# Seven of 22 FFN-up column groups as seven half-size block products instead of eight, in a one-core hybrid decoder layer

## The chip, the cores and the metric

The kernel runs on one core of a Trainium2 chip. The metric is the device time of one execution in microseconds. Its engines are TensorE (PE, with the weight loads shown apart as PEld), VectorE (DVE), ScalarE (ACT), GpSimd (POOL) and SyncE (SP); SP issues the ordinary loads, POOL issues DMAs through a software queue, and both kinds of transfer run on the same 16 DMA engines.

## The reference, cut to what matters

One decoder layer with S = 512 tokens and D = 1024 channels: an input projection, two token mixers (sparse attention and gated DeltaNet), a gated merge with an output projection, a layer norm, and then the part that is changed, a gated MLP with a causal convolution of width 3 over the tokens, followed by a second layer norm. All is float32.

```
FFN_DIM = 2816
def conv_ffn(x, w_up, conv_w, w_down):
    h = causal_dwconv(x @ w_up, conv_w)          # w_up: 1024 x 5632
    gate, val = jnp.split(h, 2, axis=-1)
    return (jax.nn.silu(gate) * val) @ w_down    # w_down: 2816 x 1024
...
        x = layer_norm(DEEPNORM_ALPHA * x + mix, ln1_g[l], ln1_b[l])
        f = conv_ffn(x, ffn_w_up[l], ffn_conv_w[l], ffn_w_down[l])
        x = layer_norm(DEEPNORM_ALPHA * x + f, ln2_g[l], ln2_b[l])
```

## The kernel before

**Products.** Every float32 operand of a product is split in two: a high part rounded to fp32r (a copy on ACT, name `wh` for weights) and a low part, the difference (a subtraction on DVE, name `wl`). A product of one 128x128 weight block is three matmuls, high by high, high by low and low by high; in `product` these are lines 484, 486 and 487. The activations of the FFN lie in SBUF as `mh` and `ml`, 8 blocks of 128 channels by 512 tokens.

**Weights.** `split_w` loads a weight tile of 512 KB (`raw`, 128x1024, a ring of three), and splits it in two halves of 128x512. `wh` and `wl` are rings of three halves each, so ACT writes a new `wh` when PE has finished with the one three halves back.

**FFN-up.** The 2816 columns of each branch (gate and value) are 22 groups of 128, so the loop `for p in range(NF)` runs over p = 0 to 21, and inside over the branches b = 0, 1. One branch of one group is 8 blocks of 128 channels by three matmuls of 512 columns, 48 matmuls in a group; they accumulate in the PSUM bank `pu0` or `pu1`. The products of groups 0 and 1 are made earlier, interleaved with the layer norm, in matmuls of 256 columns. Behind each product comes the gated convolution: ACT reads the bank (`fa`, line 1407), DVE adds two shifted terms per branch (line 1410), ACT takes the tanh, DVE and POOL multiply (lines 1415 and 1416). The result `fth` is stored split as the operand of FFN-down (`ph`, `pl`), with block sums `sr`, lines 1420 to 1430.

**FFN-down** is already done as seven block products in place of eight (the scheme of Strassen and Winograd). It needs four sums of blocks of its weights, which are made in DRAM by accumulating DMAs that POOL issues: `sums(n)`, line 513, eight DMAs of 2816 KB into `wsum`. `ROUNDS` says at which group of FFN-up each of the later ones is written in the code. The output projection `w_o` is treated the same way, with eight DMAs of 1024 KB (`osum`, line 503) in the first stage.

**Order.** The order of the instructions of each engine is written out: `QUEUES` holds one list of numbers for PE, DVE, ACT, POOL and SP each, so the work of different groups is interleaved on an engine as the lists say, not as the loop reads.

```
ROUNDS = [2, 4, 6, 8, 10, 13, 15]
BUFS = {..., 'raw': 3, 'wh': 3, 'wl': 3, ...}
```

Of the kernel before, what the change touches and what calls it, by code (L numbers as in the profile page):

```python
# [129 lines left out]
ROUNDS = [2, 4, 6, 8, 10, 13, 15]  # L130
# [3 lines left out]
    "PE": """0-9 11-12 10 13-32 41 38 35-37 33 42-43 53 39 34 54 44-45 47-48 40 50-52 49 55 46 65 56-57 66 59-60 58 61-63 67 64  # L134
71-72 77-78 74 68 79 69 89 75-76 73 70 86 90 87 80 83 91 88 98 81-82 107 101 108 99 84 109-110 100 111 85 102 112 95
113-114 96 115 103 116-117 92 118-119 93 120-122 94 97 123-148 155-178 149-153 104-106 154 183-205 207 206 208-220
179-180 221-230 181-182 235-251 259-260 252-254 261 255 262-264 231 265-267 232 302 268-271 256 303 272 257-258 233
273 234 304-305 274-277 306-307 278-282 308 310 309 311 360 283-290 361 388 291-298 362-365 389-391 366 312-313
367-370 392 371-372 314-315 373-374 393 375-377 394 378 395 379-383 396 299-300 397-405 444-446 301 447 416 406-407
417 408-410 418-419 411 420-434 456 435-436 448-449 457 437-439 458 450 316-317 451 320-321 318 322-323 319 459-463  # L140
324-327 464-466 328 332-339 329-330 467 331 468-471 513 472 340-347 473 514 474-475 348-355 476-477 515 356-359 452
384-387 516 478 517 479 501-502 453-455 412-415 518 503 519-521 504 522-526 440-441 527 442-443 723-724 528-529
725-727 530-532 728-729 480 484 481-483 533-534 485 505-506 535-536 730 486 507-508 731-733 487 734-738 751 739
488-489 752 740 490 509 491 741-742 492 541-542 753 493-494 754 743 495 510 496 543 511 546 755 497 544-545 512 547
756-757 498-499 744 758 500 548 759-760 549-551 560-561 761 745 762-765 562 565-566 766 552 767 746 553 768 554 537
555 591-592 563-564 567 538 568-569 539-540 581-582 769 570 593-596 556 597 557 598 558 599-600 770-771 559 571 583
585-586 796-797 772 584 572 798 573-575 773 587 601-602 576 799 577 774 800 588-589 801-806 603 606 590 604 651 578
605 607 579-580 807-810 608 653 811 620-621 609-611 652 812-813 654 814 612 815-816 622 625-626 613 623-624 614-616
864-865 627-628 641 629-630 642 866-870 617-618 871 619 643 645 872 631 646 873 644 632-633 874 634 875 647 876-877
635-636 699-700 648 637 649-650 638-639 878 640 701 879 704 702 880 817 705 881 703 818 882-886 706 718-719 707-709  # L150
887 720-721 819 838-839 722 710 655 659-660 656-658 661-662 840 854-855 711-712 841 663-666 842-843 713-715 856
667-669 671-678 670 857-858 716-717 844-845 679-686 860-861 859 846 862 687-694 863 1053 847-848 695-698 747-750
936-940 1054 941 1055 775 1056 776 1057 849 777-778 850 942-944 779 945-948 780 949-951 781-782 1058 952-954 783-784
1059 955 977 785 978-979 956 786-787 980 957-959 981 1060 788 1072-1073 789-790 851 982-985 791-792 986-991 793-794
992-993 795 1061 994-999 852-853 1000-1007 1074 1008-1009 1062 1075-1076 820 824-825 1010-1011 1101 821-823 826-829
1012 1102 1063 1029 830 832-833 831 1030-1036 1013 1037-1040 1103-1108 834 1014 1041 835 1042-1043 1015 836 1044 837
888-889 1045-1052 1064-1065 1016 1066-1067 1017 1077-1082 890-891 1068 1083-1100 1069 1018 1109 1070 1110 1019 1111
1020-1021 1112 1022-1024 892-894 896 895 897-899 1071 1203 1205-1208 900-903 1209 1113 1204 1114-1115 1210 1219 1116
1220 1117-1118 904 1211 908-915 905-906 1221 907 1212-1214 1223 1215 1119-1121 1216 1224 916-923 1222 1217 1122
924-931 1218 1123 932-935 1225-1226 1233-1234 960 1227 1124-1125 1228 961 1126-1127 962-963 1128-1131 964-965 1235  # L160
1132-1133 966 1134 1141-1142 967-968 1135-1136 1143-1144 969-970 1238 1145-1149 971 1236 972 1150-1151 973 1239
1179-1180 1152 1181 974 1240-1243 1237 1153-1154 975-976 1155-1156 1182 1157 1252-1253 1158-1159 1183-1184 1160
1185-1187 1161 1244 1162-1164 1188 1245-1247 1025 1137 1248 1138 1254 1139-1140 1257 1259 1026 1258 1189-1198 1273
1283 1199 1027 1249 1255 1028 1256 1250 1200 1274 1201-1202 1165 1251 1166 1260 1284-1285 1169-1170 1167 1261-1262
1168 1307-1308 1286 1309-1311 1171-1173 1275 1174 1277-1278 1287 1312 1288 1313 1263 1314-1317 1175-1176 1276 1177
1279 1178 1264 1403 1289 1404 1318 1265-1266 1405 1280-1282 1267 1408 1268 1406-1407 1269 1319 1409 1270 1320 1271
1321-1323 1290 1324 1229 1272 1291-1293 1325 1410-1411 1231 1326-1330 1294-1295 1412-1413 1422 1296 1423 1230 1297
# [1404 lines left out]
```

## Time and profile before

| what | us |
|---|---|
| median of 3 runs (lowest 832.77, highest 833.51) | 833.2 |
| the profiled execution | 831.55 |
| its span, first to last instruction | 829.8 |
| PE busy in the span | 809.2 (98%) |
| DVE busy | 602.5 (73%) |
| ACT busy | 409.2 (49%) |
| POOL busy | 180.5 (22%) |

The mean granted clock of TensorE was 0.992. The profiled execution lies 1.65 us below the median, and 1.75 us of it are outside the span. By the code and the trace the stages are: both mixers and the merge to about 432 us; the output projection, the layer norm and the first two groups of FFN-up to about 493 us; the rest of FFN-up to about 724 us; FFN-down and the last layer norm to 829.8 us. A group of instructions in the profile is named by line, engine, operation and tile; `wl<-raw,wh` is the subtraction that makes the low part of a weight.

### The profile page before, as it was taken

Reading aid. Unit: us, or ns where it says so; the run is one execution under the profiler, and the core shown is the slowest. Engines: PE = TensorE matmul, PEld = TensorE weight load, DVE = VectorE, ACT = ScalarE, POOL = GpSimd, SP = SyncE. Lnnn points to the kernel's source line nnn. Section 1 sums busy time; section 2 is a strip of 40 time slices with the busy share of each in tenths; the row PEclk is TensorE's granted clock in tenths of the full one; section 3 lists DMA queues with packets and bytes.
Section 4 is the critical chain, followed back from the end, with each engine's and each line's share of the span. In section 5 each row is a group of like instructions: output and inputs, shape, how many; then the busy total and the mean of one; then the engine's idle time right before and its main releaser. Section 6 shows DMA issues by size and latency. Waiting matters only on the chain.

```text
span 829.8 us, 11767 instructions
## 1 busy us (share of the span) xinstructions
PE 809.2 (98%) x4138; PEld 673.8 (81%) x4138; DVE 602.5 (73%) x1339; ACT 409.2 (49%) x912; POOL 180.5 (22%) x176
## 2 busy tenths in 40 slices
...
GB/s 279 102 92 101 252 32 133 44 96 108 49 219 111 233 51 52 120 108 128 115 241 177 152 147 211 125 102 102 215 103 249 229 102 80 150 199 182 190 257 124
DMA packets 43979, 119.58 MB, mean 144 GB/s; under 512 B 3472, under 2 KB 4624, under 8 KB 43664
## 3 DMA queue, kind: packets, MB, share of 16 engines
...
q0 software_dynamic: 11776, 31.46, 16.3%
q8 instruction: 33, 0.54, 0.3%
...
HBM read 116.72 MB, written 33.55 MB: 181 GB/s over the span
## 4 chain that ended last, share of the span: by engine, by line
PE 82%; DVE 9%; DMA 4%; ACT 2%; issue 2%; POOL 1%; ACTq 0%; DVEq 0%; POOLq 0%; SPq 0%
PE pu L484 10%; PE pu L486 10%; PE pu L487 10%; PE gps L484 8%; PE gps L486 8%; PE gps L487 8%; DMA raw<-wsum 3%; PE pw L1288 3%; PE px L1452 3%; PE pu L1288 2%; PE pz L1452 2%; PE pout L1089 2%; PE pu L1452 2%; PE aps L1075 2%; PE pm L484 2%
## 5 line engine op out<-in xcount | busy, mean ns | idle before, releaser
L474 DVE TENSOR_TENSOR wl<-raw,wh 128x512 fp32r<-128x512 f32 x146 | 102.7, 705 | 78.0 <-ACT wh L470 38.6
L470 ACT ACTIVATE wh<-raw 128x512 fp32r<-128x512 f32 x126 | 79.1, 629 | 133.7 <-PE pu L486 97.0
L486 PE MATMUL pu<-ml,wh 128*128 128x512 f32 (+1 forms) x384 | 131.5, 373 | 0.0
L484 PE MATMUL pu<-mh,wh 128*128 128x512 f32 (+1 forms) x384 | 130.8, 372 | 0.4 <-ACT mh L1267 0.4
L487 PE MATMUL pu<-mh,wl 128*128 128x512 f32 (+1 forms) x384 | 130.8, 373 | 0.0
L484 PE MATMUL gps<-xh,wh 128*128 128x512 f32 x320 | 125.7, 404 | 3.2 <-ACT mt L1121 2.1
L486 PE MATMUL gps<-xl,wh 128*128 128x512 f32 x320 | 126.1, 401 | 0.0
L487 PE MATMUL gps<-xh,wl 128*128 128x512 f32 x320 | 124.4, 400 | 0.0
L484 PEld LDWEIGHTS pu<-mh,wh 128*128 128x128 f32 x384 | 71.3, 188 | 13.4 <-ACT mh L1267 0.7
L487 PEld LDWEIGHTS pu<-mh,wl 128*128 128x128 f32 x384 | 71.4, 188 | 13.0 <-DVE wl L474 0.5
L486 PEld LDWEIGHTS pu<-ml,wh 128*128 128x128 f32 x384 | 71.4, 188 | 12.6
L1410 DVE SCALAR_TENSOR_TENSOR fa<-pu,fcw,fa 128x511 f32<-128x511 f32 (+1 forms) x88 | 64.6, 744 | 17.5 <-ACT fa L1407 16.9
L1416 POOL TENSOR_TENSOR fth<-fth,fa 128x512 f32<-128x512 f32 x22 | 30.4, 1387 | 212.6 <-DVE fth L1415 186.3
L484 PEld LDWEIGHTS gps<-xh,wh 128*128 128x128 f32 x320 | 60.4, 190 | 15.1 <-issue 2.5
L487 PEld LDWEIGHTS gps<-xh,wl 128*128 128x128 f32 x320 | 60.8, 190 | 10.9
L486 PEld LDWEIGHTS gps<-xl,wh 128*128 128x128 f32 x320 | 61.0, 191 | 10.2
L1387 ACT ACTIVATE wh<-raw 128x512 fp32r<-128x512 f32 x67 | 40.1, 626 | 41.0 <-DMA raw<-in_down 13.5
L1388 DVE TENSOR_TENSOR wl<-raw,wh 128x512 fp32r<-128x512 f32 x67 | 44.8, 694 | 17.9 <-ACT wh L1387 17.3
L474 POOL TENSOR_TENSOR wl<-raw,wh 128x512 fp32r<-128x512 f32 x30 | 40.1, 1339 | 13.4 <-ACT wh L470 7.9
L525 POOL TENSOR_TENSOR rs<-rs,minus_half 128x1 f32<-128x1 f32 x8 | 7.2, 901 | 161.4 <-DVE rs L1246 161.4
L1407 ACT ACTIVATE fa<-pu,fcw 128x512 f32<-128x512 f32 x44 | 29.7, 680 | 24.8 <-PE pu L487 22.0
L1048 ACT ACTIVATE sc<-sc,mn 128x384 f32<-128x384 f32 (+2 forms) x64 | 35.7, 560 | 10.5 <-DVE mn L1046 10.1
(365 smaller groups left out, 1719.8 us busy)
## 6 DMA issues: line engine op xcount, KB each, us to landing
raw<-in_up SPq DMA_DIRECT2D x44, 512.0 KB, 3.7
raw<-in_wT SPq DMA_DIRECT2D x40, 512.0 KB, 3.6
wsum<-in_down POOLq DMA_DIRECT2D x6, 2816.0 KB, 20.8
raw<-wsum SPq DMA_DIRECT2D x20, 512.0 KB, 3.9
raw<-in_down SPq DMA_DIRECT2D x15, 512.0 KB, 4.3
...
wsum<-wsum POOLq DMA_DIRECT2D x2, 2816.0 KB, 14.6
raw<-in_wm SPq DMA_DIRECT2D x8, 512.0 KB, 3.5
```

What stands on the lines that cost most here:

```text
L470: A.activation(wh, r, AF.Copy)
L474: eng.tensor_tensor(wl, r, wh.bitcast(F32), op=OP.subtract)
L484: i = PE.matmul(ps, wh[k], mh_(k), start=(k == 0), stop=False)
L486: PE.matmul(ps, wh[k], ml_(k), start=False, stop=False)
L487: PE.matmul(ps, wl[k], mh_(k), start=False, stop=(k == n - 1))
L1048: A.activation(s[:, i, :n], s[:, i, :n], AF.Exp, scale=-1.0, bias=mn[:, 0, i:i + 1], accum_out=mn[:, 1, i:i + 1])
L1288: PE.matmul(ps[t], a[x](j)[:, ts], w[y][:, j % 2, :], start=fresh and j == 0 and i == 0, stop=j == TT - 1 and i == 2, skip_group_check=True)
L1387: A.activation(hi, raw[:, i], AF.Copy)
L1388: V.tensor_tensor(lo, raw[:, i], hi.bitcast(F32), op=OP.subtract)
L1410: V.scalar_tensor_tensor(acc[:, n:], ps[:, :S - n], w[:, i:i + 1], acc[:, n:], op0=OP.mult, op1=OP.add)
L1416: G.tensor_tensor(th, th, g[1], op=OP.mult)
L1452: m = PE.matmul(ps, a[x][:, j, ts], w[y], start=first and i == 0, stop=last and i == 2, skip_group_check=True)
```

## The change

Groups 5, 7, 9, 11, 13, 15 and 17 of FFN-up are taken as one product of 2x2 blocks each: the activations in two halves of the channels by two halves of the tokens (`x11`, `x12`, `x21`, `x22`, each 4 channel blocks by 256 tokens), the weights in two halves of the channels by the two branches. `seven(p)` makes seven products of 4 channel blocks by three matmuls of 256 columns, 84 matmuls of 256 columns in place of 48 of 512. It is a generator in four pieces that are written between the four half products of the plain group p - 1.

- Weights: of the seven weight blocks three are blocks of `ffn_w_up`, and four are sums, which eight accumulating DMAs of POOL prepare in DRAM for all seven groups (`sums_u`, 1.8 MB each). A group loads 1.75 MB in place of 1 MB and splits seven halves of 128x512 in place of four. Two of the four loads of a group go into a tile of its own, `raw7`, which has one buffer: weights 0 and 1 first, and later 4 and 5.
- Activations: `x_sums` makes four sums of blocks and splits them, once, written between groups 1 and 2: ten operations on DVE (six sums and four splits), two on POOL and four copies on ACT, all 128x1024.
- Results: partial results are combined in SBUF (`wf0`, `wf1`): four copies of 128x256 on ACT and three additions of 128x256 on DVE for a group. The gated convolution of these groups then reads SBUF in place of a PSUM bank.
- The tiles `ph`, `pl` and `sr` are cut in a part for 9 and a part for 2 of the 11 pairs of groups, the second of which is allocated when the tiles of the seven-product groups are freed; later pieces of `sr` are split 5, 4, 2 in place of 4, 4, 3.
- `ROUNDS` and all lists of `QUEUES` are new. The eight `wsum` DMAs move: before, three stood in the first stage and five in FFN-up; now all stand behind the first stage or in FFN-up, and the eight DMAs of `sums_u` stand in the first stage among those of `osum`.

```diff
-ROUNDS = [2, 4, 6, 8, 10, 13, 15]
+SEVEN = [5, 7, 9, 11, 13, 15, 17]
+NA = 9
+ROUNDS = [2, 4, 6, 8, 10, 12, 14]
...
 QUEUES = {
-    "PE": """0-9 11-12 10 13-32 41 38 35-37 33 42-43 53 39 34 54 44-45 47-48 40 50-52 49 55 46 65 56-57 66 59-60 58 61-63 67 64
...
+    usum = dr.tile([128, len(SEVEN), 4, S + 16], F32, name="usum")[:, :, :, :S]
+    def u_block(r, c):
+        a, n = SEVEN[0], len(SEVEN)
+        return d["up"][a:a + 2 * n:2, :, c, 4 * r:4 * r + 4, :].rearrange("u p k f -> p u (k f)")
+    def sums_u():
+        at = lambda i: usum[:, :, U_AT[i], :]
+        todo = [(0, u_block(0, 0), 0), (1, u_block(0, 1), 0), (0, u_block(0, 1), 1), (1, u_block(1, 1), 1),
+                (2, at(1), 0), (2, u_block(0, 0), 1), (3, at(2), 0), (3, u_block(1, 0), 1)]
+        for (to, src, add), u in zip(todo, SUMS_U):
+            i = G.dma_start(out=at(to), in_=src, **({"accum_op": OP.add} if add else {}))
...
+    def x_sums():
...
+        def parts_of(i, x):
+            A.activation(xs_[i][0], x, AF.Copy)
+            V.tensor_tensor(xs_[i][1], x, xs_[i][0].bitcast(F32), op=OP.subtract)
+        a, b, c, e = spare
+        G.tensor_tensor(a, hi(x11), lo(x11), op=OP.add)
+        V.tensor_tensor(b, hi(x21), lo(x21), op=OP.add)
+        V.tensor_tensor(c, b, hi(x22), op=OP.subtract)
+        V.tensor_tensor(c, c, lo(x22), op=OP.subtract)
+        parts_of(0, c)
+        V.tensor_tensor(e, c, a, op=OP.subtract)
+        parts_of(1, e)
+        G.tensor_tensor(b, a, b, op=OP.subtract)
+        parts_of(2, b)
+        V.tensor_tensor(c, e, hi(x12), op=OP.add)
+        V.tensor_tensor(c, c, lo(x12), op=OP.add)
+        parts_of(3, c)
...
+    def seven(p):
...
+        def weights(i):
+            if i % 2 == 0:
+                own = i in (0, 4)
+                raws[i] = raw = (sx if own else wp).tile([128, 2, 512], F32, name="raw7" if own else "raw",
+                                                         bufs=1 if own else BUFS["raw"])
...
+                if i == 0:
+                    nc.sync.dma_start(out=raw, in_=flat(0, 0, 8))
+                elif i == 2:
+                    nc.sync.dma_start(out=raw, in_=usum[:, n, 0:2, :])
+                elif i == 4:
+                    nc.sync.dma_start(out=raw[:, 0:1], in_=usum[:, n, 2:3, :])
+                    nc.sync.dma_start(out=raw[:, 1:2], in_=flat(1, 4, 8))
+                else:
+                    nc.sync.dma_start(out=raw[:, 0:1], in_=usum[:, n, 3:4, :])
...
+        mul(0, px, pure_(x11), True)
+        A.activation(f[0][:, left_], px[:, :256], AF.Copy)
+        yield
+        mul(1, py, pure_(x12), True)
+        V.tensor_tensor(f[0][:, left_], f[0][:, left_], py[:, :256], op=OP.add)
+        mul(2, px, sum_(1), False)
+        A.activation(f[1][:, left_], px[:, :256], AF.Copy, scale=-1.0)
+        yield
+        mul(3, pz, sum_(0), True)
+        A.activation(f[1][:, right_], pz[:, :256], AF.Copy)
+        mul(4, px, sum_(2), False)
+        V.tensor_tensor(f[1][:, right_], f[1][:, right_], px[:, :256], op=OP.subtract)
+        yield
+        mul(5, pz, sum_(3), False)
+        V.tensor_tensor(f[1][:, left_], f[1][:, left_], pz[:, :256], op=OP.add)
+        mul(6, px, pure_(x22), False)
+        A.activation(f[0][:, right_], px[:, :256], AF.Copy)
+        yield f
...
     for p in range(NF):
+        if p == NE:
+            x_sums()
         g = []
+        if p in SEVEN:
+            f = next(ahead)
+            g = [gated(p, b, f[b]) for b in range(2)]
+        elif p + 1 in SEVEN:
+            ahead = seven(p + 1)
         for b in range(2):
...
-                wu = split_w(d["up"][p, :, b], [128, KD, 128], V)
-                i = product(ps, wu, (lambda k: mh[:, k, :], lambda k: ml[:, k, :]), KD)
+                for half in range(2):
+                    if p + 1 in SEVEN and (b or half):
+                        next(ahead)
+                    i = plain(p, b, half, ps) or i
```

In the rows below the names are those of the code, with a number for the buffer; `waits` names the semaphores that an instruction waits for.

PE in the middle of FFN-up, before: the matmuls of one branch, in triples, with some of the next branch mixed in.

```order
L486 MATMUL pu_5744<-ml,wh 128x512
L487 MATMUL pu_5744<-mh,wl 128x512
L484 MATMUL pu_5744<-mh,wh 128x512
L486 MATMUL pu_5744<-ml,wh 128x512
L487 MATMUL pu_5744<-mh,wl 128x512
L487 MATMUL pu_5698<-mh,wl 128x512
```

PE in the middle of FFN-up, after: lines 1515 (the seven-product groups) and 1568 (plain groups).

```order
L1568 MATMUL pu_5920<-mh,wl 128x512
L1568 MATMUL pu_5920<-mh,wh 128x512
L1568 MATMUL pu_5920<-ml,wh 128x512
L1568 MATMUL pu_5920<-mh,wl 128x512
L1515 MATMUL px_5703<-ml,wh 128x256
L1515 MATMUL px_5703<-mh,wl 128x256
L1515 MATMUL px_5939<-mh,wh 128x256
L1515 MATMUL px_5939<-ml,wh 128x256
L1515 MATMUL px_5939<-mh,wl 128x256
```

Matmuls of 512 columns now alternate with runs of 256 columns that go to other banks.

DVE in the loop of FFN-up, before: low parts of weights (line 474) between the convolution terms (1410) and the gate (1415).

```order
L1410 SCALAR_TENSOR_TENSOR fa_6030<-pu_6004,fcw,fa_6030 128x511
L1415 SCALAR_TENSOR_TENSOR fth<-fth,fa_5942 128x512 [waits DVE_49]
L474 TENSOR_TENSOR wl<-raw,wh 128x512 [waits PE_49,Activation_49]
L1410 SCALAR_TENSOR_TENSOR fa_6069<-pu_6044,fcw,fa_6069 128x511
L1410 SCALAR_TENSOR_TENSOR fa_6069<-pu_6044,fcw,fa_6069 128x510 [waits DVE_49]
L1410 SCALAR_TENSOR_TENSOR fa_6030<-pu_6004,fcw,fa_6030 128x510
L474 TENSOR_TENSOR wl<-raw,wh 128x512 [waits DMAHW6_49,PE_49,Activation_49]
```

DVE in the loop of FFN-up, after: 1505 makes the low parts for a seven-product group (`raw_6056` is its weights 0 and 1 or 4 and 5 in `raw7`, `raw_6180` the next content of the same tile), 1563 those of a plain group, 1534, 1537 and 1527 are the additions into `wf`.

```order
L1505 TENSOR_TENSOR wl<-raw_6056,wh 128x512 [waits DMAHW5_49,PE_49,Activation_49]
L1563 TENSOR_TENSOR wl<-raw,wh 128x512 [waits PE_49,Activation_49]
L1505 TENSOR_TENSOR wl<-raw_6056,wh 128x512 [waits DMAHW6_49,PE_49,Activation_49]
L1534 TENSOR_TENSOR wf_5943<-wf_5943,px_5939 128x256 [waits PE_49]
L1505 TENSOR_TENSOR wl<-raw,wh 128x512 [waits DMAHW7_49,Activation_49]
L1607 SCALAR_TENSOR_TENSOR fth<-fth,fa_5903 128x512 [waits Activation_49]
L1563 TENSOR_TENSOR wl<-raw,wh 128x512 [waits DMAHW0_49,PE_49,Activation_49]
L1537 TENSOR_TENSOR wf_5943<-wf_5943,pz_5941 128x256
L1505 TENSOR_TENSOR wl<-raw_6180,wh 128x512 [waits DMAHW1_49,PE_49,Activation_49]
```

Seven low parts and three additions of a group are woven into the work of the plain group; between the last low part from one content of `raw7` and the first from the next stand five other instructions of DVE, two of them low parts.

POOL from the layer norm into FFN-up, before: one step of the inverse square root, then the gates `fth`, with two weight-sum DMAs among them.

```order
L525 TENSOR_TENSOR rs<-rs,minus_half 128x1 [waits DVE_49,Pool_49] x2
L513 DMA wsum_101<-in_down 1408x1x512 [waits DMASW2_49]
L1416 TENSOR_TENSOR fth<-fth,fa_5461 128x512 [waits DVE_49,Activation_49]
L1416 TENSOR_TENSOR fth<-fth,fa_5446 128x512
L513 DMA wsum_102<-wsum_101 1408x512 [waits DMASW3_49]
L1416 TENSOR_TENSOR fth<-fth,fa_5550 128x512 [waits DVE_49,Activation_49]
```

POOL in the same place, after: lines 1440 and 1447 are the two operations of `x_sums`, 1608 is the gate.

```order
L539 DMA wsum_101<-in_down 1408x1x512 [waits DMASW2_49,DMASW1_49]
L1440 TENSOR_TENSOR sr0a<-mh,ml 128x1024 [waits DMAHW1_49,DVE_49,DMAHW3_49,PE_49,Activation_49]
L1447 TENSOR_TENSOR sr1a<-sr0a,sr1a 128x1024 [waits DVE_49,Pool_49]
L1608 TENSOR_TENSOR fth<-fth,fa_5481 128x512 [waits DVE_49,Activation_49]
L539 DMA wsum_102<-wsum_101 1408x512 [waits DMASW2_49]
L1608 TENSOR_TENSOR fth<-fth,fa_5466 128x512
L1608 TENSOR_TENSOR fth<-fth,fa_5586 128x512 [waits DVE_49,Activation_49]
L539 DMA wsum_102<-in_down 1408x1x512 [waits DMASW4_49,DMASW3_49]
L1608 TENSOR_TENSOR fth<-fth,fa_5671 128x512 [waits DVE_49,Activation_49]
L1608 TENSOR_TENSOR fth<-fth,fa_5907 128x512 [waits DVE_49,Pool_49]
L539 DMA wsum_100<-in_down 1408x1x512 [waits DMASW0_49]
```

The weight-sum DMAs now follow one another with one to two gates between them in the first groups of FFN-up, where before the next one stood several gates on.

More of the change, by code (lines that the diff above doesn't have):

```diff
@@ L139 @@
[L139 to L143, printed above, removed]
@@ L517, in gemm_t @@
         ps = gps()
-        first = product(ps, w, (lambda k: xh[:, k, :], lambda k: xl[:, k, :]), KD)
+        FIRST[u] = first = product(ps, w, (lambda k: xh[:, k, :], lambda k: xl[:, k, :]), KD)
         if after is not None:
@@ L1142, in body @@
     sums_o()
+    sums_u()
     tail = ExitStack()
@@ L1369, in body @@
     pdn = psum("pdn", 1)
+    sxs = ExitStack()
+    sx = pool(sxs, name="sx", bufs=1, side="left")
+    xs_ = [tuple(sx.tile([128, 4, 256], F32R, name=f"s{x}{i}") for x in "hl") for i in range(4)]
+    x11, x12, x21, x22 = ((k, slice(256 * r, 256 * r + 256)) for r in range(2) for k in range(2))
+    def x_sums():
+        spare = [r.js(NA - 4, NA) for r in sr]
+        hi, lo = (lambda v: mh[:, 4 * v[0]:4 * v[0] + 4, v[1]].bitcast(F32)), (
+            lambda v: ml[:, 4 * v[0]:4 * v[0] + 4, v[1]].bitcast(F32))
+        def parts_of(i, x):
[14 more added lines that the diff above has]
+        parts_of(3, c)
     soon = []
@@ new lines, in gated, with plain @@
+    def gated(p, b, ps):
+        w = fcw[:, b * NF + p, :]
+        acc = fs.tile([128, S], F32, name=f"fa{b}", bufs=2)
+        A.activation(acc, ps, AF.Copy, scale=w[:, 2:3])
+        for i in (1, 0):
+            n = 2 - i
+            V.scalar_tensor_tensor(acc[:, n:], ps[:, :S - n], w[:, i:i + 1], acc[:, n:],
+                                   op0=OP.mult, op1=OP.add)
+        return acc
+    raws_ = {}
+    def plain(p, b, half, ps):
+        if half == 0:
+            raws_[b] = wp.tile([128, KD, 128], F32, name="raw", bufs=BUFS["raw"])
+            nc.sync.dma_start(out=raws_[b], in_=d["up"][p, :, b])
+        r = raws_[b][:, 4 * half:4 * half + 4]
+        hi = wp.tile([128, 4, 128], F32R, name="wh", bufs=BUFS["wh"])
+        lo = wp.tile([128, 4, 128], F32R, name="wl", bufs=BUFS["wl"])
+        A.activation(hi, r, AF.Copy)
+        V.tensor_tensor(lo, r, hi.bitcast(F32), op=OP.subtract)
+        m = None
+        for j in range(4):
+            k = 4 * half + j
+            for i, (w, x) in enumerate(((hi, mh), (hi, ml), (lo, mh))):
+                q = PE.matmul(ps, w[:, j], x[:, k, :], start=k == 0 and i == 0, stop=k == KD - 1 and i == 2,
+                              skip_group_check=True)
+                m = m or q
+        return m if half == 0 else None
```

527 lines of the change are left out of this document (298 added, 229 removed).

## The prediction

> **What bounds the kernel now.** I read the page's head and its chain first, then the span cut into the four stages, then single instructions of PE and DVE in the stage that changes, the waits there, and the DMA rows. Busy times and the chain:
>
> ```profile
> PE 809.2 (98%) x4138; PEld 673.8 (81%) x4138; DVE 602.5 (73%) x1339; ACT 409.2 (49%) x912; POOL 180.5 (22%) x176
> PE 82%; DVE 9%; DMA 4%; ACT 2%; issue 2%; POOL 1%; ACTq 0%; DVEq 0%; POOLq 0%; SPq 0%
> ```
>
> PE is the bound of the whole. The stages, each with its length, then busy time and count of PE, PEld, DVE, ACT and POOL, granted clock, DMA share, GB/s; the last row is the inside of the third:
>
> ```profile
> 0.00:432.00 432.00, 420.57 (x2335) 352.33 (x2336) 310.43 (x871) 232.39 (x625) 136.09 (x141) 0.99 0.42 126
> 432.00:493.00 61.00, 60.55 (x365) 53.58 (x364) 52.47 (x83) 26.37 (x36) 5.06 (x5) 1.00 0.56 158
> 493.00:724.00 231.00, 231.00 (x1027) 190.85 (x1027) 153.10 (x249) 100.32 (x173) 33.81 (x25) 1.00 0.54 152
> 724.00:829.80 105.80, 97.11 (x417) 77.05 (x415) 86.51 (x138) 50.07 (x81) 5.50 (x5) 0.98 0.60 191
> 508.00:720.00 212.00, 212.00 (x934) 174.82 (x933) 142.60 (x233) 93.87 (x161) 29.55 (x22) 1.00 0.54 154
> ```
>
> From 493 to 724 PE is busy 231.00 of 231.00 us at clock 1.00: a microsecond of PE work removed here is a microsecond of the span, until something else is late. DVE has 142.60/212 = 67%. The waits of that stage (engine and line waiting, then what it waited for: total us, times, longest) say how much room the others leave:
>
> ```profile
> ACT wh L470 <- PE pu L486: 95.0, 57, 5.4
> PEld pu L487 <- DVE wl L474: 0.5, 2, 0.3
> ```
>
> The weight splits wait for PE (through the ring of `wh`), PE hardly ever for them. So the room there is what the change spends.
>
> **The change, part by part.** First the matmuls. Starts of consecutive matmuls of 512 columns in the stage, and of 256 columns (groups 0 and 1 today):
>
> ```profile
> 530.18 0.39 PE L484 MATMUL pu<-mh,wh 128*128 128x512 f32 x1
> 530.41 0.39 PE L486 MATMUL pu<-ml,wh 128*128 128x512 f32 x1
> 530.63 0.39 PE L487 MATMUL pu<-mh,wl 128*128 128x512 f32 x1
> ...
> 487.06 0.28 PE L487 MATMUL pu<-mh,wl 128*128 128x256 f32 x1
> 487.18 0.28 PE L484 MATMUL pu<-mh,wh 128*128 128x256 f32 x1
> 487.30 0.28 PE L487 MATMUL pu<-mh,wl 128*128 128x256 f32 x1
> ```
>
> The listed 0.39 and 0.28 overlap; the step from start to start counts. It is 212/934 = 0.227 us for 512 columns and 0.120 for 256. A group costs 48 x 0.227 = 10.90 us before and 84 x 0.120 = 10.08 after: 0.82 less, 5.7 us for seven. Seven products of eight would be 1.36 less; the fixed part of the shorter matmul takes 0.54 of it. Bounds: exact if both steps hold.
>
> The Trainium skill, "TensorE: Matmul & The Clock Gate", section "Back-to-back issue gap", speaks against the change: it gives a sustained spacing, set by matmul and weight load together, of about 81 ns at 128 columns and 131 ns at 512. A straight line between them (an estimate from that page) is 98 ns at 256, so 84 x 98 = 8.2 us against 48 x 131 = 6.3: a group would be 1.9 us longer and the kernel 13 us. The trace's steps of 0.227 and 0.120 lie far from these, so I put the row in the sum.
>
> Where the two sizes mix, as they now do in every pair of a plain and a seven-product group, the start after a 512 comes a 512's step later:
>
> ```profile
> 493.30 0.40 PE L484 MATMUL pu<-mh,wh 128*128 128x512 f32 x1
> 493.53 0.28 PE L487 MATMUL pu<-mh,wl 128*128 128x256 f32 x1
> ```
>
> 0.23, which two decimals don't tell from 0.227. With some 14 changes of size in a pair and at most 0.01 each, seven pairs lose 0 to 1.0; I take +0.5.
>
> `x_sums`: 10 DVE operations of 128x1024, and the low parts of all the weights beside them. The nearest rows are a pair of 128x1024 subtractions, and the small operations of the loop:
>
> ```profile
> 449.95 2.48 DVE L1175 TENSOR_TENSOR wol<-raw,woh 128x1024 fp32r<-128x1024 f32 x2
> ...
> 512.65 0.68 DVE L474 TENSOR_TENSOR wl<-raw,wh 128x512 fp32r<-128x512 f32 x1
> 513.25 1.40 DVE L1410 SCALAR_TENSOR_TENSOR fa<-pu,fcw,fa 128x511 f32<-128x511 f32 x2
> 514.57 0.41 DVE L1429 TENSOR_TENSOR sr<-sr,fth 128x256 f32<-128x256 f32 x1
> 514.90 0.68 DVE L474 TENSOR_TENSOR wl<-raw,wh 128x512 fp32r<-128x512 f32 x1
> ...
> 493.00:532.00 39.00, 39.00 (x182) 32.30 (x182) 22.54 (x35) 14.25 (x25) 5.01 (x4) 1.00 0.66 191
> ...
> 480.50 1.79 POOL L513 DMA_DIRECT2D wsum<-in_down  x1
> L1416 POOL TENSOR_TENSOR fth<-fth,fa 128x512 f32<-128x512 f32 x22 | 30.4, 1387 | 212.6 <-DVE fth L1415 186.3
> ```
>
> 10 x 1.24 = 12.4 us come into a stretch where DVE has 39.00 - 22.54 = 16.5 us free; PE uses the first sum near 523 and the last near 532 (groups 2 and 3 take 21.8 us behind 493, and the products of group 5 are woven into group 4). It fits with 4 us over, except at moments when a weight's low part stands behind a long operation. Bounds 0 and 3 (two such operations in the way, 2.48); I take +0.5. The four copies on ACT lie beside PE. The two sums on POOL, some 2 x 1.39 us each, stand behind a `wsum` DMA that waits for an earlier one to land; the same DMA was issued at 480.50 before, ahead of the time the sums can start, and POOL has 5.01 us of work in these 39: nothing.
>
> DVE from group 4 to 18: by starts, one low part costs 0.60, one convolution term 0.66, one 128x256 operation 0.33. A pair has 11 low parts (was 8), 8 terms, 2 gates, 3 new additions and 2.25 us of `pl` and `sr`: 6.6 + 5.3 + 1.2 + 1.0 + 2.25 = 16.3 us in 10.90 + 10.08 = 20.98, 78%; by listed durations about 18.4, 88%. PE has stayed full above that:
>
> ```profile
> 440.00:460.00 20.00, 20.00 (x90) 16.57 (x89) 19.63 (x30) 9.86 (x12) 0.92 (x1) 1.00 0.62 193
> 460.00:480.00 20.00, 20.00 (x139) 18.25 (x138) 20.00 (x34) 6.51 (x9) 1.85 (x3) 1.00 0.38 123
> ```
>
> DVE 19.63 and 20.00 of 20 us, PE 20.00. I cost this at nothing; bounds 0 and 3. ACT rises by three copies and four evictions for a pair, about 0.7 us each as in the row of `fa`:
>
> ```profile
> L1407 ACT ACTIVATE fa<-pu,fcw 128x512 f32<-128x512 f32 x44 | 29.7, 680 | 24.8 <-PE pu L487 22.0
> ```
>
> From 93.87/212 = 44% it goes to some 66%: nothing. An eviction adds a wait for PE, since the next product into the same bank follows it; but between two products of one bank stand another product and a plain half, 1.44 + 2.72 = 4.2 us, against 0.7 of eviction. That wait is covered unless ACT or DVE is 3 us behind.
>
> Loads. `raw7` has one buffer: the load of its next content waits, on SP's queue, for the last low part made from the old one; behind it wait the other weights' loads, in order. Until PE needs the new content it has, for the step from weight 5 to the next group's weight 0, the products 5 and 6 and one plain half, 2 x 1.44 + 2.72 = 5.6 us, and about 1 us by which DVE runs ahead (an estimate: a low part and a term); for the step from weight 1 to 4 the products 1 to 3 and one plain half, 7.0, and the same 1. A load's landing, first without and then beside an accumulating DMA:
>
> ```profile
> raw<-in_up SPq DMA_DIRECT2D x3, 512.0 KB, 3.5
> ...
> raw<-in_up SPq DMA_DIRECT2D x3, 512.0 KB, 7.7
> ...
> 578.11 1.73 POOL L513 DMA_DIRECT2D wsum<-in_down  x1
> wsum<-in_down POOLq DMA_DIRECT2D x6, 2816.0 KB, 20.8
> wsum<-wsum POOLq DMA_DIRECT2D x2, 2816.0 KB, 14.6
> L470 ACT ACTIVATE wh<-raw 128x512 fp32r<-128x512 f32 x126 | 79.1, 629 | 133.7 <-PE pu L486 97.0
> ```
>
> (The first is from 520 to 540 us, the next from 580 to 600, just behind the DMA of 578.11.) With the copy, 0.63, and the low part, 0.68, the chain is 4.8 us at best, under both covers: no stall. Beside an accumulating DMA it is 9.0: 2.4 late for weight 0 and 1.0 late for weight 4. Five such DMAs, of 14.6 to 20.8 us, now fall among the 147 us of the seven pairs: half of the time, so 3.5 steps of either kind, 3.5 x 3.4 = 11.9 us if all stall whole. Bounds 0 and 11.9. I take a quarter, +3.0: the DMAs of 20.8 don't load the queues evenly, and ACT and DVE can lead where they waited 95.0 us for PE before.
>
> The first stage. Eight DMAs of 1.8 MB enter, three of 2.8 MB leave, and all orders are new. What such a change can touch there:
>
> ```profile
> 98.12 4.52 DVE L1013 TENSOR_TENSOR cs<-cs,csm 128x512 f32<-128x512 f32 x1
> 98.50 1.35 POOL L653 TENSOR_TENSOR vraw<-th,acc 128x512 f32<-128x512 f32 x1
> 102.69 0.33 PE L659 MATMUL aps<-ident,cs 128*128 128x128 f32 x1 [2.97 <-DVE tiny L578]
> 400.00:432.00 32.00, 29.94 (x125) 24.29 (x124) 16.99 (x32) 9.27 (x19) 4.19 (x4) 0.95 0.49 179
> 406.09 0.47 PE L484 MATMUL gps<-xh,wh 128*128 128x512 f32 x1 [2.06 <-ACT mt L1121]
> ```
>
> A DVE operation of 0.7 us took 4.52 beside POOL's, and PE stood 2.97 us behind it; in 400 to 432 PE ran at clock 0.95 after an idle of 2.06, another 32 x 0.05 = 1.6 us. One such place costs 2.97 + 1.6 = 4.6; the new order can remove one or make one. Bounds -4.6 and +4.6; in the new order the rows of `tiny` stand earlier and no `osum` DMA stands beside `cs`, so I take -1.0.
>
> FFN-down has the same operations on cut tiles, moved by a few rows. Its sums come later: the last `wsum` DMA was issued here,
>
> ```profile
> 638.78 1.71 POOL L513 DMA_DIRECT2D wsum<-in_down  x1
> ```
>
> and now about 25 us later (an estimate from its place behind the gates); with 20.8 us it lands near 685, 40 us ahead of FFN-down. 0, bounds -1 and +1.
>
> Sum: -5.7 + 0.5 + 0.5 + 0 + 3.0 - 1.0 + 0 = -2.7 against the profiled 831.55 (span 829.8 and 1.75 around it): 828.85. The median of the runs lies 1.65 higher, so the forecast for the median is 833.2 - 2.7 = **830.5 us**.
>
> **The rivals.** A: slower, by the exchange of `raw7`. If each step beside an accumulating DMA stalls whole, +11.9 stands in place of +3.0: -2.7 + 8.9 = +6.2, 839.4. For it: one buffer, and a landing of 7.7; against it: a POOL order that leaves such a DMA out of the middle of the steps. It decides from stalls of 3.0 + 2.7 = 5.7 us in sum, 0.8 a group. Each idle of PE can also lower the clock, as the row of 400 to 432 shows.
>
> B: no change, about 833: DVE at 78 to 88% and the long operations of `x_sums` take 2.5 us more in small waits (of their bounds of 3 each). For it: the order on DVE is tight; against it: the rows with DVE at 98 and 100%.
>
> C: the full gain: no stall at `raw7`, and the place of `cs` gone: -5.7 + 0.5 + 0.5 - 4.6 = -9.3, 823.9.
>
> D: weight loads bind. PEld's 174.82/933 = 0.187 us each would make 84 x 0.187 = 15.7 us a group, +4.8, seven times: 867. Against it stands the step of 0.120 with a weight load for each matmul. The rule of the Trainium skill named above ("Back-to-back issue gap") points to this side, with a smaller price.
>
> That the saved matmuls do not reach the end is excluded by 231.00 of 231.00, as long as PE stays full.
>
> **How the numbers follow.** Forecast 0.46 (its own range 828.0 to 831.5), A 0.25, B 0.18, C 0.08, D 0.03. A measurement of this kernel tells about 0.2%, 1.7 us, from no change. Faster: the forecast, C and 0.03 of B, whose waits may be shorter: 0.57. Same: the other 0.15 of B and 0.03 of A, where the stalls just eat the gain: 0.18. Slower: 0.22 of A and D: 0.25. The range takes the forecast and B, the half of C above 825.5, and the half of A under 838, 0.46 + 0.18 + 0.04 + 0.12 = 0.80: 825.5 to 838.
>
> **What would show it.** 84 matmuls at steps of 0.120 in the pairs, 0.227 in plain groups (else D). PE 100% busy from 493 on; idle moments ahead of line 1515 with `wh` or `wl` of `raw7` as releaser, and loads landing in 7 us or more there, are A. Long waits of PE for line 1505 or 1563 behind line 1441 to 1449 are B. The idle of 2.97 us near 102 us gone is C. The prediction is wrong if PE's share of the FFN-up stage falls under 98%.

## The result: 0.7% slower, and the profile after

Six runs of the changed kernel have a median of 838.53 us (836.19 to 840.48), six of the kernel before beside them 833.15; the ratio is 1.007, 95% interval 1.0051 to 1.0089. The forecast was 830.5, range 825.5 to 838.0; the time is just above it, and near the 839.4 of rival A.

The page of the kernel after, busy times and the chain by engine:

```profile
span 835.7 us, 12479 instructions
PE 806.7 (97%) x4390; PEld 681.9 (82%) x4390; DVE 641.3 (77%) x1391; ACT 432.1 (52%) x965; POOL 195.2 (23%) x186
PE 77%; DVE 10%; DMA 7%; ACT 3%; issue 2%; POOL 0%; SPq 0%; DVEq 0%; ACTq 0%; POOLq 0%
```

PE is still the bound, but the chain now runs through DMA for 7% of the span (4% before). The same stretches as before (length; busy time and count of PE, PEld, DVE, ACT, POOL; granted clock; DMA share; GB/s):

```profile
0.00:432.00 432.00, 421.90 (x2352) 353.76 (x2353) 316.19 (x875) 234.64 (x630) 142.56 (x147) 1.00 0.52 146
432.00:493.00 61.00, 59.84 (x363) 52.47 (x362) 50.79 (x78) 24.18 (x31) 5.73 (x6) 1.00 0.76 219
493.00:724.00 231.00, 221.59 (x1226) 191.05 (x1225) 183.18 (x293) 118.05 (x217) 39.35 (x27) 0.99 0.67 181
724.00:829.80 105.80, 103.37 (x454) 84.65 (x452) 88.35 (x142) 55.29 (x90) 6.61 (x5) 1.00 0.62 191
```

In FFN-up PE is busy 221.59 of 231.00 us, where it was 231.00: 96%, under the 98% that the prediction named as its own refutation. To place the loss, take four matmuls that both kernels have: the last of the merge (`pm`), of the transposes of the layer norm (`pt`), of FFN-up (`pu`) and of FFN-down (`px`). The rows of before, then of after (start and duration; the end is their sum):

```profile
429.81 0.39 PE L487 MATMUL pm<-yoh,wl 128*128 128x512 f32 x1
484.70 0.49 PE L1265 MATMUL pt<-ident,x 128*128 128x128 f32 x3
720.53 0.39 PE L487 MATMUL pu<-mh,wl 128*128 128x512 f32 x1
821.49 0.39 PE L1452 MATMUL px<-w,pl 128*128 128x512 f32 x1
```

```profile
426.09 0.39 PE L498 MATMUL pm<-yoh,wl 128*128 128x512 f32 x1
483.47 0.49 PE L1292 MATMUL pt<-ident,x 128*128 128x128 f32 x3
729.17 0.39 PE L1568 MATMUL pu<-mh,wl 128*128 128x512 f32 x1
827.75 0.39 PE L1645 MATMUL px<-w,plb 128*128 128x512 f32 x1
```

| stretch | before | after | change | predicted |
|---|---|---|---|---|
| to the end of the merge | 430.2 | 426.5 | -3.7 | -1.0 |
| to the last transpose | 55.0 | 57.5 | +2.5 | 0 |
| FFN-up to its last matmul | 235.7 | 245.6 | +9.9 | -1.7 |
| FFN-down | 101.0 | 98.6 | -2.4 | 0 |
| tail | 7.9 | 7.6 | -0.3 | 0 |

The table compares the two profiled executions (831.55 and 837.50 us). A second profile of the changed kernel, taken beside the later runs (833.22 us), has 425.3, 57.1, 243.6, 97.9 and 7.6 us for the same stretches, so a stretch of one profile is good to about 2 us.

FFN-up is 11.6 us over its forecast, and the other stretches together give 2.9 back. PE's idle rows in FFN-up, of 0.25 us and more here and below (in brackets: idle before, and what released it):

```profile
545.97 0.39 PE L1515 MATMUL px<-sh,wh 128*128 128x256 f32 x1 [1.79 <-ACT wf L1524]
562.24 0.50 PE L1568 MATMUL pu<-mh,wh 128*128 128x512 f32 x1 [1.17 <-ACT wh L1562]
563.76 0.80 PE L1568 MATMUL pu<-mh,wl 128*128 128x512 f32 x1 [0.79 <-DVE wl L1563]
579.22 0.39 PE L1515 MATMUL px<-sh,wh 128*128 128x256 f32 x1 [1.20 <-ACT wh L1504]
586.78 0.36 PE L1515 MATMUL px<-mh,wh 128*128 128x256 f32 x1 [0.92 <-DVE wf L1534]
589.85 0.50 PE L1568 MATMUL pu<-mh,wh 128*128 128x512 f32 x1 [1.05 <-ACT wh L1562]
625.20 0.39 PE L1515 MATMUL px<-sh,wh 128*128 128x256 f32 x1 [2.04 <-ACT wf L1529]
```

Seven places, 8.96 us, before none. Three kinds of cause stand behind them.

The load. At 625 ACT's eviction is late because a weight copy in front of it waited for a load; the chain there (start, us, what), and ACT's rows:

```profile
615.76 0.61 DVE wl L1505
616.39 7.75 DMA raw<-usum
```

```profile
624.24 0.63 ACT L1504 ACTIVATE wh<-raw 128x512 fp32r<-128x512 f32 x1 [3.76 <-DMA raw<-usum]
624.78 0.37 ACT L1529 ACTIVATE wf<-px 128x256 f32<-128x256 f32 x1
```

The load of weight 4 starts when DVE has made the last low part from weights 0 and 1 in `raw7` (615.76), and lands 7.75 us later: the exchange of the one buffer, as the prediction described it.

The buffer of `wf`. At 546 PE waits for an eviction (the copy of a finished product out of its PSUM bank), and that waits for DVE, which still reads the last group's `wf` for its convolution. The product was complete near 541.8 and its eviction began at 545.53; from 540 to 546 DVE is busy 5.78 of 6.00 us. DVE and then ACT:

```profile
543.70 0.74 DVE L1548 SCALAR_TENSOR_TENSOR fa<-wf,fcw,fa 128x511 f32<-128x511 f32 x1
544.37 0.42 DVE L1622 TENSOR_TENSOR sr1a<-sr0a,fth 128x256 f32<-128x256 f32 x1
544.70 0.74 DVE L1548 SCALAR_TENSOR_TENSOR fa<-wf,fcw,fa 128x510 f32<-128x510 f32 x1
545.53 0.38 ACT L1524 ACTIVATE wf<-px 128x256 f32<-128x256 f32 x1 [1.03 <-DVE fa L1548]
```

At 579 two causes meet: ACT's eviction waits for DVE to read `wf`, and the copy of weight 4 behind it for a load that landed at 578.5, 7.4 us after its issue.

```profile
578.01 0.38 ACT L1529 ACTIVATE wf<-px 128x256 f32<-128x256 f32 x1 [2.84 <-DVE fa L1548]
578.53 0.63 ACT L1504 ACTIVATE wh<-raw 128x512 fp32r<-128x512 f32 x1
```

The order. At 562 the copy that PE needs (561.56) stands on ACT behind a store of the gate's result that waits 3.02 us for POOL:

```profile
560.18 0.63 ACT L1619 ACTIVATE pha<-fth 128x512 fp32r<-128x512 f32 x1 [3.02 <-POOL fth L1608]
560.72 0.67 ACT L1545 ACTIVATE fa<-pu,fcw 128x512 f32<-128x512 f32 x1
561.29 0.37 ACT L1539 ACTIVATE wf<-px 128x256 f32<-128x256 f32 x1
561.56 0.63 ACT L1562 ACTIVATE wh<-raw 128x512 fp32r<-128x512 f32 x1
```

After two of the idle places, from 546.45 and from 563.52, the granted clock is 0.50 for 3.41 us each, though PE has work:

```profile
546.00:556.00 10.00, 10.00 (x54) 8.80 (x55) 4.78 (x9) 3.54 (x7) 0.00 (x0) 0.83 0.95 229
556.00:566.00 10.00, 8.05 (x42) 6.59 (x41) 6.10 (x11) 4.62 (x10) 4.27 (x3) 0.88 0.79 199
```

```profile
547.68 0.41 PE L1515 MATMUL px<-sh,wl 128*128 128x256 f32 x1
547.90 0.41 PE L1515 MATMUL px<-sh,wh 128*128 128x256 f32 x1
...
548.75 0.63 PE L1568 MATMUL pu<-mh,wl 128*128 128x512 f32 x1
549.18 0.41 PE L1515 MATMUL px<-sl,wh 128*128 128x256 f32 x1
```

In these two stretches a matmul of 256 columns steps on after 0.213 us and one of 512 after 0.43, in place of 0.120 and 0.227; 17 such steps cost 2.5 us.

The sum for FFN-up closes. By the written order 992 matmuls of 512 columns and 85 of 256 lie between the last transpose and the last matmul of FFN-up before, 657 and 665 after: at 0.227 and 0.120 that is 235.4 us before (measured 235.7) and 228.9 after (measured 245.6). Of the 16.7 us over it, 8.96 are idle, 2.5 half-clock steps, 1.2 matmuls that step a little wider where sizes mix, and about 4 are single steps that are longer by over 0.06 us without being listed as idle (the first matmuls behind an idle step by 0.34 in place of 0.227, and waits under 0.25).

### The profile page after: what moved, and what is told of

Same layout as the page of the kernel before. It is cut to its first block, busy times and chain, and to the rows that moved or that the text cites. A ratio compares the mean times of both kernels' runs of the same rounds, so it can differ in the third digit from the quotient of the medians.

```text
span 835.7 us, 12479 instructions
## 1 busy us (share of the span) xinstructions
PE 806.7 (97%) x4390; PEld 681.9 (82%) x4390; DVE 641.3 (77%) x1391; ACT 432.1 (52%) x965; POOL 195.2 (23%) x186
## 4 chain that ended last, share of the span: by engine, by line
PE 77%; DVE 10%; DMA 7%; ACT 3%; issue 2%; POOL 0%; SPq 0%; DVEq 0%; ACTq 0%; POOLq 0%
PE pu L1568 15%; PE gps L495 8%; PE gps L497 8%; PE gps L498 8%; PE px L1645 4%; PE px L1515 4%; PE pz L1645 4%; PE pz L1515 3%; DMA raw<-in_up 2%; PE pout L1115 2%; PE aps L1101 2%; DMA raw<-usum 2%; PE pu L1645 2%; PE pm L495 2%; PE pm L497 2%
## 5 line engine op out<-in xcount | busy, mean ns | idle before, releaser
L1568 PE MATMUL pu<-mh,wh 128*128 128x512 f32 x208 | 80.4, 398 | 2.2 <-ACT wh L1562 2.2
L1568 PE MATMUL pu<-mh,wl 128*128 128x512 f32 x208 | 79.7, 399 | 1.0 <-DVE wl L1563 1.0
L1568 PE MATMUL pu<-ml,wh 128*128 128x512 f32 x208 | 79.8, 396 | 0.0
L1608 POOL TENSOR_TENSOR fth<-fth,fa 128x512 f32<-128x512 f32 x22 | 32.4, 1474 | 197.3 <-DVE fth L1607 150.6
L485 DVE TENSOR_TENSOR wl<-raw,wh 128x512 fp32r<-128x512 f32 x66 | 48.4, 738 | 29.7 <-PE gps L498 13.6
L1470 ACT ACTIVATE wh<-raw 128x512 fp32r<-128x512 f32 x67 | 39.9, 626 | 38.9 <-PE px L1645 9.5
L1562 ACT ACTIVATE wh<-raw 128x512 fp32r<-128x512 f32 x52 | 32.6, 628 | 51.5 <-PE pu L1568 41.5
L1471 DVE TENSOR_TENSOR wl<-raw,wh 128x512 fp32r<-128x512 f32 x67 | 44.4, 691 | 16.7 <-ACT wh L1470 16.6
L1563 DVE TENSOR_TENSOR wl<-raw,wh 128x512 fp32r<-128x512 f32 x52 | 38.2, 739 | 21.3 <-ACT wh L1562 18.1
L1504 ACT ACTIVATE wh<-raw 128x512 fp32r<-128x512 f32 x49 | 30.6, 628 | 40.2 <-PE px L1515 15.2
L1548 DVE SCALAR_TENSOR_TENSOR fa<-pu,fcw,fa 128x511 f32<-128x511 f32 (+1 forms) x60 | 44.3, 745 | 7.7 <-ACT fa L1545 7.4
L481 ACT ACTIVATE wh<-raw 128x512 fp32r<-128x512 f32 x46 | 28.8, 627 | 38.4 <-PE gps L497 29.6
L1568 PEld LDWEIGHTS pu<-mh,wh 128*128 128x128 f32 x208 | 39.7, 191 | 8.8 <-ACT wh L1562 2.6
L1568 PEld LDWEIGHTS pu<-mh,wl 128*128 128x128 f32 x208 | 39.6, 191 | 8.8 <-DVE wl L1563 2.6
L1568 PEld LDWEIGHTS pu<-ml,wh 128*128 128x128 f32 x208 | 39.6, 190 | 6.2
```

What stands on the lines that cost most here:

```text
L485: eng.tensor_tensor(wl, r, wh.bitcast(F32), op=OP.subtract)
L1470: A.activation(hi, raw[:, i], AF.Copy)
L1471: V.tensor_tensor(lo, raw[:, i], hi.bitcast(F32), op=OP.subtract)
L1548: V.scalar_tensor_tensor(acc[:, n:], ps[:, :S - n], w[:, i:i + 1], acc[:, n:], op0=OP.mult, op1=OP.add)
L1562: A.activation(hi, r, AF.Copy)
L1563: V.tensor_tensor(lo, r, hi.bitcast(F32), op=OP.subtract)
```

## The experiments

Theories at that point: L, the loads of `raw7` beside the accumulating DMAs; W, the single buffer of `wf`; O, the written order of ACT and DVE. All ratios are to the kernel before, run on the same chip; as not all kernels ran on one chip, two changed kernels are compared by their ratios. The changed kernel itself, again beside some of the later ones, gave 1.0068 (1.0045 to 1.0090), as in the first comparison.

> The changed kernel again, as the yardstick beside the others on this chip: 1.005 to 1.009 of the kernel before, merge ends near 426.5 us, FFN-up idle of PE 8 to 10 us.

**No accumulating DMAs for FFN-down.**

```diff
     def sums(n, after):
+        return
...
+    wsum = [w_block(0, 0), w_block(0, 1), w_block(1, 0), w_block(1, 1)]
```

> The changed kernel without the eight accumulating DMAs of the FFN-down weight sums; FFN-down reads plain blocks of its weights in their place (so its sums are left out). Theory L (the loads of raw7 and of the sums land late beside these DMAs): the two stalls that the trace of the changed kernel shows behind a load (1.20 us near 579 and 2.04 near 625) go, and the half-clock stretches with them: 838.5 - 3 to - 5 = 833.5 to 835.5, loads land in under 5 us. Theory W (the single buffer of wf holds ACT's evictions until DVE has read the old content): the stalls near 544 and 579 stay, at most 1 us gained: 837.5 or more. Theory O (the written order of DVE and ACT is too tight, whatever the loads do): 837 to 838.5, the stalls ahead of lines 1515 and 1568 stay with other releasers.

1.0009 (0.9987 to 1.0031), about 5 us better than the change. The stall at 625 is gone; the idle of FFN-up is 6.2 us, and the waits that stay are those of W and O (PE's waits from 493 to 730; total us, times, longest):

```profile
PE pu L1568 <- ACT wh L1562: 2.2, 2, 1.2
PE px L1515 <- ACT wf L1524: 1.8, 1, 1.8
PE px L1515 <- ACT wh L1504: 1.0, 1, 1.0
PE px L1515 <- DVE wf L1534: 0.9, 1, 0.9
```

The stall near 579 stayed (0.98 us, behind the same eviction), so the load alone had not caused it, other than theory L had it.

**Two buffers of `raw7`.**

```diff
-                                                         bufs=1 if own else BUFS["raw"])
+                                                         bufs=2 if own else BUFS["raw"])
...
+    xs_.insert(1, (sx.tile([128, 4, 256], F32R, name="sh1"), xs_[0][1]))
```

> raw7 with two buffers; to make room the low parts of two of the four sums of activations share a tile (one low part is left out). Theory L: the exchange of raw7 no longer waits for the last low part of the old content, the stalls near 579 and 625 (3.2 us) go: 834 to 836. Theory W and theory O: 837.5 to 839.

1.0016 (1.0003 to 1.0028), 4.3 us better than the change with all accumulating DMAs in place. The two stretches of FFN-up, first of the change and then of this kernel:

```profile
540.00:600.00 60.00, 53.09 (x302) 45.49 (x301) 42.02 (x71) 28.29 (x54) 6.91 (x5) 0.94 0.83 198
600.00:680.00 80.00, 77.50 (x480) 68.81 (x479) 61.74 (x107) 44.41 (x84) 10.93 (x9) 1.00 0.52 165
```

```profile
540.00:600.00 60.00, 53.60 (x312) 45.74 (x311) 43.34 (x74) 28.41 (x55) 6.90 (x5) 0.97 0.80 192
600.00:680.00 80.00, 79.93 (x489) 71.22 (x489) 65.45 (x113) 46.73 (x87) 14.84 (x11) 1.00 0.55 173
```

From 600 to 680 PE is full again. That one of the two half-clock stretches is missing from 540 to 600 is not shown to come from `raw7`: the stall of 1.79 us ahead of it is still there, and the second profile of the change lacks the stretch too. Taking away the traffic and taking away the exchange give the same within the intervals: what cost was the one buffer together with a landing of 7 us or more. Of the 4.3 us, 2.04 are seen as idle behind a load at 625 and 0.5 at 579 (1.20 to 0.70); the rest was not placed.

**Two buffers of `wf`.**

```diff
-        f = [fs.tile([128, S], F32, name=f"wf{b}", bufs=1) for b in range(2)]
+        f = [fs.tile([128, S], F32, name=f"wf{b}", bufs=2) for b in range(2)]
```

> wf0 and wf1 with two buffers each; room as in the run with two buffers of raw7, and two tiles of FFN-down lie elsewhere. Theory W: the stall of 1.79 near 544 and part of the 1.20 near 579 go, and the half-clock stretch at 546 to 556 that followed: 838.5 - 3 to - 5 = 833.5 to 835.5. Theory L: the stall near 544 shrinks by under 1 us, 837.5 or more. Theory O: 837.5 to 839, the stall moves to the next tight place.

1.0045 (1.0029 to 1.0061), about 2 us better than the change, with intervals that overlap. The stall of 1.79 fell to 0.65, that near 579 stayed at 1.19, now behind the load alone:

```profile
576.79 0.63 ACT L1505 ACTIVATE wh<-raw 128x512 fp32r<-128x512 f32 x1 [2.83 <-DMA raw<-usum]
```

So at 579 either cause is enough, and the kernel with both buffers (next) has no stall there.

**Both.** Two of the sums' low parts also change places on DVE.

> raw7 and wf with two buffers each; two pairs of the sums' low parts share a tile. If L and W hold together and add up: FFN-up's idle of PE falls from 9 to under 4 us and the clock stays at 1.00: 838.5 - 5 to - 8 = 830.5 to 833.5. If O holds: 836.5 or more, PE idle in FFN-up still 6 us or more, with low parts of weights or gates as releasers.

0.9989 (0.9975 to 1.0002): the gains add (0.52%, 0.23% and together 0.79%). Against two buffers of `raw7` alone, on the same chip, the second `wf` gives 0.27%, 2.2 us, with intervals that just do not overlap: W is real, and smaller than L. The idle of FFN-up is 4.9 us, none of it behind a load; the longest waits of PE are 1.2 us for a weight copy on ACT and 0.9 for an addition into `wf` on DVE.

**Both, without the accumulating DMAs.** The edits of the first and the fourth run together.

> Two buffers of raw7 and wf, and the accumulating DMAs of the FFN-down sums left out (FFN-down reads plain blocks): what the loads still cost once the exchange has two buffers. Theory L says nothing more is lost to loads: within 1.5 us of the kernel with both buffers, 0.997 to 1.000, the same stalls near 544, 559, 583 and 586. If late loads still feed those stalls: 0.993 to 0.996.

0.9973 (0.9957 to 0.9989), 1.3 us better than with both buffers, with the intervals overlapping; idle 4.6 us, most of it at the same places. With two buffers the DMAs cost little.

**Both, and five instructions moved.** One of the four moves on ACT, and the one on DVE:

```diff
 L1608 ACTIVATE fth<-fa_5901 128x512
-L1621 ACTIVATE pha<-fth 128x2x256
 L1547 ACTIVATE fa_6090<-pu_5982,fcw 128x512
 L1541 ACTIVATE wf_5940<-px_5937 128x256
 L1564 ACTIVATE wh<-raw 128x512
 L1506 ACTIVATE wh<-raw_6178 128x512
+L1621 ACTIVATE pha<-fth 128x2x256
...
-L1507 TENSOR_TENSOR wl<-raw,wh 128x512
 L1536 TENSOR_TENSOR wf_6177<-wf_6177,px_6173 128x256
+L1507 TENSOR_TENSOR wl<-raw,wh 128x512
```

> The kernel with two buffers of raw7 and wf, and five instructions moved in the written order (four on ACT, one on DVE): a store of the gate's result behind the next weight copies, an addition into wf ahead of a low part, a weight copy ahead of a gate, an eviction ahead of a weight copy. Theory O for what is left after the buffers (PE idle 4.9 us in six places and half-clock near 558, released by ACT or DVE, none by a load): the idle falls under 2 us and the time by 3 to 6 us against the kernel with both buffers: 0.992 to 0.996 of the kernel before. If the places are only symptoms of too much work on DVE, the idle moves elsewhere and the ratio stays at 0.998 to 1.000.

0.9976 (0.9961 to 0.9991), 1 us better than before the moves with intervals that overlap, less than the 3 to 6 expected, with 4.0 us of idle. Where the store had stood, the next instruction (`fa<-pu`) now waited 3.24 us for PE to finish its bank, with the same weight copy behind it. ACT there:

```profile
557.65 0.69 ACT L1547 ACTIVATE fa<-pu,fcw 128x512 f32<-128x512 f32 x1 [3.24 <-PE pu L1570]
```

Three of the four places left now wait for a low part on DVE (0.92, 0.96 and 1.11 us). That is nearer to the expectation's other reading, too much work on DVE, than to theory O; no run took work off DVE, so how much of this rest is order and how much is work stays open.

**The early order alone**, in the kernel before: all engines' lists up to the end of the merge from the change, the rest as before.

> The kernel before, with the changed kernel's order of all engines up to the end of the merge (426 us), the three early accumulating DMAs of wsum behind that place and no DMAs for the sums of FFN-up. If the first stage's gain of 3.7 us comes from its new order alone: the merge ends near 426.5 in place of 430.2, and the whole is 2 to 4 us shorter, 0.995 to 0.998. If it came from something that the seven-product groups bring: merge end 429 or later, 0.999 to 1.002.

The merge ended at 426.4 us, so the gain needs nothing of the seven-product groups. It is not shown to be the order alone: the early `wsum` DMAs moved with it (the first is issued at 400 us, in the kernel before at 81). The whole was 1.0090 (1.0069 to 1.0111), since at the seam of the two lists, just behind, PE stands idle up to 4.30 us for a single wait, 9 us in sum; this total says nothing on the order.

```profile
425.98 0.39 PE L485 MATMUL pm<-yoh,wl 128*128 128x512 f32 x1
...
442.82 0.50 PE L1286 MATMUL pw<-woh,ah 128*128 128x512 f32 x1 [4.30 <-ACT woh L1172]
```

**Two DMAs later.** `wsum` DMAs of groups 8 and 11 moved on POOL behind the last exchange; all else as in the change.

> The changed kernel, nothing but two accumulating DMAs of wsum moved on POOL, from the gates of groups 8 and 11 to those behind the last exchange of raw7 (near 650 and 675 us); one buffer of raw7 and wf as in the change. Theory L: the two stalls behind raw7 near 575 and 621 (1.0 and 1.3 us here, 1.2 and 2.0 in the first profile) go, with what the lowered clock costs behind them: 1.002 to 1.0045 of the kernel before, as with two buffers of raw7 (1.0016). If only the buffer and not the accumulating traffic matters: 1.006 to 1.008.

1.0051 (1.0031 to 1.0071): 1.4 us better than the change, with intervals that overlap, and between the two expectations. The stall at 621 to 625 is gone, but the DMA issued at 692.87 occupies POOL for 1.72 us just ahead of a gate, for which ACT and DVE wait with PE's next weights behind. The other two kernels with the late DMAs (below) have a stall of 2.0 and 2.4 us at this place, those without them none. Rows of POOL, DVE and PE:

```profile
692.87 1.72 POOL L539 DMA_DIRECT2D wsum<-in_down  x1 [13.70 <-DVE wl L1563]
695.94 1.48 DVE L1614 TENSOR_TENSOR sr2a<-fth 128x256 f32<-128x256 f32 x1 [2.51 <-POOL fth L1608]
698.08 0.50 PE L1568 MATMUL pu<-mh,wl 128*128 128x512 f32 x1 [1.87 <-DVE wl L1563]
```

**The change's buffers with the late DMAs and more moves.** Six instructions moved on ACT and six on DVE (the expectation counts thirteen).

> The kernel with the two late DMAs and thirteen instructions of ACT and DVE moved by a few places each; all buffers as in the change, nothing left out. Theory O for the rest: FFN-up idle of PE falls from 8 to 9 us to under 4, 0.996 to 0.9995 of the kernel before. If the idle only moves to other places: 1.000 to 1.003.

1.0011 (0.9995 to 1.0027), 6.3 us of idle in eight places: the moves are worth 0.40%, 3.3 us, against the kernel with only the late DMAs, on the same chip and with intervals that do not overlap.

**Everything, with and without the late DMAs.**

> Two buffers of raw7 and wf, the two late DMAs, and the moves of ACT and DVE: 0.993 to 0.997 of the kernel before, PE idle in FFN-up under 3 us. If the moves give nothing beyond those of the kernel with five: 0.997 to 0.999.

> Two buffers of raw7 and wf, the moves of ACT and DVE, and the accumulating DMAs of wsum where the change has them. If the two late DMAs of the kernel with all three only shifted a stall to 690 us (2.4 us there): FFN-up near 235 us in place of 237.6, 0.9945 to 0.997 of the kernel before. If the moves beyond the first five give nothing: 0.997 to 0.999.

With the late DMAs 0.9979 (0.9961 to 0.9997), without them 0.9973 (0.9961 to 0.9986). The moves beyond the first five give nothing that can be told. Both, like the kernel with five moves, are faster than the kernel before, by 0.2 to 0.3%, and than the change, but their second buffers have room only because low parts of the sums are left out. The kernel with the change's own buffers and nothing left out (1.0011) is only level with the kernel before.

## Why the prediction was wrong, point by point

- **Matmul time (-5.7): right.** Steps of 0.119 and 0.227 to 0.233 us; the count of matmuls explains FFN-up in both kernels as shown above. 235.4 - 228.9 = 6.5, of which 5.7 is the seven groups; the rest is what of groups 0 and 1 now lies ahead of the last transpose. Rival D (weight loads) is refuted by the steps of 0.119. The Trainium skill, "TensorE: Matmul & The Clock Gate", section "Back-to-back issue gap", gives a sustained spacing of about 131 ns at 512 columns; the trace disagrees with it, at 227 ns.
- **Mixing of sizes (+0.5): mis-sized, 1.2,** just over its bound of 1.0. In the mixture 512 columns step by 0.232 on average, and the size changes some 39 times in a pair, where I had counted 14.
- **`x_sums` (+0.5): no cost was seen.** While it ran, PE was full:

```profile
490.00:540.00 50.00, 50.00 (x277) 43.47 (x276) 44.63 (x60) 25.29 (x44) 13.28 (x8) 1.00 0.73 197
```

- **DVE and ACT "at nothing" (bounds 0 and 3): the step that failed.** I compared shares (78 to 88%) with two rows in which PE stayed full at 98 and 100% of DVE, and I let the eviction's wait be "covered unless ACT or DVE is 3 us behind". They were (3.8 us at 546, from 541.8 to 545.53): ACT waits in its own order, for POOL's gate, for DVE's reads of `wf`, and holds the next weight copy. Six of the seven idle places, 6.9 of 8.96 us, are of this kind; at one of them, 579, a load was late too. I had not listed the wait that the one buffer of `wf` adds at all: an eviction now waits for the convolution of the group before. By the runs, `wf` is worth 0.23 to 0.27%, about 2 us, and the order some 3 us with the change's buffers. With both second buffers and the moves, 4 us of idle stay whose cause is open.
- **Exchange of `raw7` (+3.0): the mechanism right, mis-sized.** It is worth 4.3 us (1.0068 to 1.0016) or, by taking the DMAs away, 4.9, within the bounds of 0 and 11.9. The steps that met a late load were 1 to 4 (2.04 us at 625, and 579), which I had put at 1.0 late, and not 5 to 0. Three accumulating DMAs were issued among the seven pairs (at 531, 560 and 610), not the five of the sum.
- **Idle has a second price.** I added the lost clock in rival A in one sentence without a number, and in FFN-up's forecast not at all: 2.5 us, and 4 us in slow restarts and short waits, came on top of 9 us of idle. The half-clock part differs from one execution to the next: the second profile has one such stretch in FFN-up, the first two.
- **First stage (-1.0): -3.7 at the end of the merge, -1.2 at the last transpose.** The idle of 2.97 us near 100 is gone, and of three half-clock stretches of 3.41 us in this stage (near 103, 171 and 407) one is left (403). The run with the early order shows that the gain needs no DMAs for the sums of FFN-up; order and the later `wsum` DMAs were not separated (one of the eight is still issued in this stage, at 400.5). Of the 2.5 us more behind it, about 0.7 is the work of groups 0 and 1 just named and 0.7 is idle (1.16 us against 0.45); the rest was not taken apart.
- **FFN-down (0): -2.4.** PE is idle for 0.77 us in both; matmul steps longer by over 0.06 us than 0.227 are 16 before, 2.2 us in sum, and 4 after, 0.5 us. With the new code of this stage it took 97.4 to 99.6 us in nine kernels here that compute it in full, with the old one 101.0 and 100.4; the order is the likely cause, the cut tiles are a rival that was not tried.

Rival A had the sign and nearly the time (839.4), by stalls at `raw7` alone; in fact these are less than half, and the rest is its neighbour B (small waits of DVE and ACT), which I had priced at 2.5 us. The two add up, and I had given them as alternatives; that A's number came so near is luck.
